# Windowed attention on one core: value products in two sets of three PSUM banks, row sums first, and an earlier second load wave

## The chip, the cores and the metric

The kernel runs on one core of a Trainium2 chip. A core has a matrix engine (TensorE, PE in the profile; its weight loads are listed as PEld), a vector engine (VectorE, DVE), a scalar engine (ScalarE, ACT), GpSimd (POOL) and SyncE (SP). They run their own instruction streams and meet at semaphores. Sixteen DMA engines carry data between the DRAM of the chip (HBM) and the on-chip memory (SBUF). Matrix results land in PSUM, which has eight banks of 128 partitions by 512 fp32 values. The metric is device time in microseconds (us) of one execution; lower is better.

## The reference

Inputs q, k and v are fp32 of shape (4, 4096, 1536). The sequence is cut into windows of 64 rows; each window attends to itself only.

```python
q_w = q.reshape(B, nw, W, D)          # B=4, nw=64, W=64, D=1536
k_w = k.reshape(B, nw, W, D)
v_w = v.reshape(B, nw, W, D)
logits = np.einsum('bnwd,bnud->bnwu', q_w, k_w) * D ** -0.5
attn = np.exp(logits - logits.max(-1, keepdims=True))
attn = attn / attn.sum(axis=-1, keepdims=True)
out = np.einsum('bnwu,bnud->bnwd', attn, v_w)
```

Each of q, k, v and out has 16384 rows of 1536 fp32 values, 100.7 MB. Reading three and writing one moves 402.7 MB.

## The kernel before

**Units.** The 16384 rows are cut into N = 32 units of 512 rows. Each partition of an SBUF tile holds SLOTS = 4 rows of the unit. Loads of q, k and v go through GpSimd's DMA queue and cast to fp16 on the way (3.146 MB read, 1.573 MB written). The result of a unit is scaled into one of three fp32 tiles `outs` and stored by one 3.146 MB DMA. So in the steady state each unit asks for four DMAs of 3.146 MB on the DRAM side: q, k, store and v, in that order on the one queue.

**One unit on the engines.** PE transposes q in six groups and k in six groups (L142), always pairs of fp16 values as one fp32, into two PSUM banks `tps` in turn; DVE copies the even groups to SBUF and ACT the odd ones (`copy_out`, L219). The score products (L160) go to two banks `lts`, one for each half h of the unit. ACT takes the exponential of the 32x32 blocks (L265) into `ets`, fp16. There is no subtraction of the maximum. Then come four value products, n = 0 to 3 (n = 2h + t): each multiplies two weight blocks of `ets` by v16, with 3 column blocks j of 512, accumulated over r = 0 and 1, into three PSUM banks `ops`. One more product per n, with a column of ones, gives the row sums (`sp`). DVE takes the reciprocal of the sums (L241); the scaled eviction of the six (n, j) with n + j even is on ACT (L276), of the other six on DVE (L250).

**Banks.** All four value products write the same three banks `ops`. The first matmul into a bank (r = 0) waits on `f_o[j][n % 2]`, which the eviction of the product before gives back (`told`). The eight banks are: two `tps`, two `lts`, three `ops`, one `sp`.

**Order of DMA work.** It is written out by hand on POOL and SP. For unit u, POOL waits for `m_q` (a small matmul after the last q transpose of the unit, L151) and issues the load of q for u+1; waits for `m_k` (a score product after the last k transpose) and issues the load of k; waits for `m_0` (value product n = 0 of the unit has begun its second half) and issues the store of unit u-1; waits for `m_v` (last value matmul) and issues the load of v. SP waits for the loads in order and hands each to PE (`g_q`, `g_k`, `g_v`).

**Start.** SP loads q of unit 0 raw (fp32) in two DMAs of two slots each into `outs[0]`; DVE and ACT cast it. When the first of the two has landed (`d_r0`), POOL issues k and v of unit 0, makes the identity matrix, and issues q, k, v of unit 1 and v of unit 2, some of them into spare halves of `outs`, from where POOL later copies them (`unstage`, L290).

**End.** v of the last unit is loaded early into `vs` and copied by DVE (L238). The store of unit 30 waits for `n_e`, a mark that DVE and ACT set after unit 30. The last unit is stored in five pieces: half h = 0 (1.573 MB) after `m_2`, slot 2 (0.786 MB) after `m_3`, both on POOL's queue, and slot 3 in three pieces of 0.262 MB from SP (L402), one after each eviction.

Of the kernel before, what the change touches and what calls it, by code (L numbers as in the profile page):

```python
# [11 lines left out]
P = 128  # L12
# [5 lines left out]
def kernel(  # L18
# [31 lines left out]
    def sem(name):  # L50
# [21 lines left out]
    d_r0, d_r1, d_q, d_k, d_v, d_vs, d_q1, d_k1, d_v1 = (  # L72
        sem(n) for n in ("d_r0", "d_r1", "d_q", "d_k", "d_v", "d_vs", "d_q1", "d_k1", "d_v1")
    )
    d_o = [sem(f"d_o{i}") for i in range(NO)]
    d_l = [sem(f"d_l{i}") for i in range(5)]
# [3 lines left out]
    f_o = [[sem(f"f_o{j}{i}") for i in range(2)] for j in range(NJ)]  # L80
# [6 lines left out]
    m_q, m_k, m_v, m_0, m_2, m_3 = (sem(n) for n in ("m_q", "m_k", "m_v", "m_0", "m_2", "m_3"))  # L87
# [44 lines left out]

    def tensor_unit():
        def transpose(g):
            src = q16 if g < DC else k16
            c = g % DC
            for i in range(SLOTS):
                r, j = i // H, i % H
                pairs = src[:, R * j + r, :].bitcast(FP32)
                if g % DC == 0 and i == 0:  # L140
                    await_(nc.tensor, g_k if g else g_q)
                ins = nc.tensor.transpose(  # L142
                    tps[g % 2][:, r, j, :], pairs[:, c * P : (c + 1) * P], ident[:, :]
                )
                if i == 0 and g >= 2:
                    ins._wait_ge(f_c[(g - 2) % 4], 1).then_inc(f_c[(g - 2) % 4], -1)
                if i == SLOTS - 1:
                    ins.then_inc(p_t[g % 2], 1)
            if g == DC - 1:

                nc.tensor.matmul(  # L151
                    lts[0][:, 0, 0, 0:1], lhsT=ets[0][:, 0, 0, :], rhs=ones[:, 0:1],
                    start=True, stop=True, skip_group_check=True,
                ).then_inc(m_q, 1)

        def product(c):
            for h in range(H):
                for w in range(2):
                    for r in range(R):
                        ins = nc.tensor.matmul(  # L160
                            lts[h][:, r, :, :],
                            lhsT=halves(xk, c)[:, r, h, :, w],
                            rhs=halves(xq, c)[:, :, h, :, w],
                            start=(c == 0 and w == 0 and r == 0),
                            stop=(c == DC - 1 and w == 1),
                            skip_group_check=True,
                        )
                        if h == w == r == 0 and c >= DC - 2:
                            s = f_c[(DC + c) % 4]
                            ins._wait_ge(s, 1).then_inc(s, -1)  # L170
                        if h == w == r == 0 and c == DC - 3:
                            ins.then_inc(m_k, 1)
                        if c == DC - 1 and w == r == 1:
                            ins.then_inc(p_l, 1)

        for g in range(2 * DC):
            transpose(g)
            if g >= DC + 2:
                product(g - DC - 2)
        product(DC - 2)  # L180
        product(DC - 1)
        for n in range(H * R):
            h, t = n // R, n % R
            if n == 0:
                await_(nc.tensor, g_v)
            for r in range(R):
                w = ets[h][:, r, t, :]
                ld = nc.tensor.ldweights(w)  # L188
                if r == 0 and t == 0:
                    ld._wait_ge(f_x[h], 1)  # L190

                at = NJ - 1 if n == H * R - 1 else 1
                for j in range(NJ):
                    ins = reuse(
                        ops[j][:, :], w, v16[:, R * h + r, 512 * j : 512 * (j + 1)], r == 0, r == R - 1
                    )
                    if r == 0:
                        ins._wait_ge(f_o[j][n % 2], 1).then_inc(f_o[j][n % 2], -1)
                    elif j > at:
                        ins.then_inc(p_o[on_act(n, j)], 1)  # L200
                    elif j == 0 and n != 1:
                        ins.then_inc({0: m_0, 2: m_2, 3: m_3}[n], 1)
                    elif j == NJ - 1:
                        ins.then_inc(m_v, 1)
                    if j == at:
                        ins = reuse(sp[:, n : n + 1], w, ones[:, 0:1], r == 0, r == R - 1)
                        if r == 0 and t == 0:
                            ins.then_inc(f_x[h], -1)
                        if r == R - 1:
                            ins.then_inc(p_s, 1)  # L210
# [4 lines left out]
    def copy_out(eng, copy, g):  # L215
        xt = xq if g < DC else xk
        await_(eng, p_t[g % 2])
        dst = xt[:, g % DC, :].rearrange("p (r e j) -> p r j e", r=R, j=H)
        copy(out=dst, in_=tps[g % 2][:, :, :, :]).then_inc(f_c[g % 4], 1)  # L219
# [5 lines left out]
    def told(ins, u, n, j, a):  # L225
        if u == N - 1 and n == H * R - 1:
            ins.then_inc(n_e[a], 1)
        else:
            ins.then_inc(f_o[j][(n + 1) % 2], 1)

    def vector_unit(u):
        ve = nc.vector
        for g in range(0, 2 * DC, 2):
            copy_out(ve, ve.tensor_copy, g)
        if u == N - 1:
            ve.wait_ge(d_vs, 32)
            ve.wait_ge(m_v, N - 1)
            ve.tensor_copy(out=v16[:, :, :], in_=vs[:, :, :]).then_inc(g_v, 1)  # L238
        for n in range(H * R):
            await_(ve, p_s)  # L240
            ve.reciprocal(out=rs[:, n : n + 1], in_=sp[:, n : n + 1]).then_inc(n_d, 1)  # L241
            await_(ve, n_d)
            ve.sem_inc(n_r, 1)  # L243
            if n == 0:
                await_(ve, fr[0])
            for j in range(NJ):
                if not on_act(n, j):
                    if j == NJ - 1 and n != H * R - 1:
                        await_(ve, p_o[0])
                    ins = ve.tensor_scalar_mul(  # L250
                        scaled(u, n, j), ops[j][:, :], scalar1=rs[:, n : n + 1]
                    )
                    told(ins, u, n, j, 0)
        if u == N - 2:
            ve.memset(zeros[:, 1:2], 0.0).then_inc(n_e[0], 1)

    def scalar_unit(u):
# [12 lines left out]
        for n in range(H * R):  # L270
            await_(sc, n_r)
            for j in range(NJ):
                if on_act(n, j):
                    if j == NJ - 1:
                        await_(sc, p_o[1])
                    ins = sc.activation(  # L276
                        scaled(u, n, j), ops[j][:, :], COPY, bias=0.0, scale=rs[:, n : n + 1]
                    )
                    told(ins, u, n, j, 1)
        if u == N - 2:  # L280
            sc.copy(out=zeros[:, 2:3], in_=zeros[:, 0:1]).then_inc(n_e[1], 1)
# [12 lines left out]
    with tc.tile_critical(no_gpsimd_drain=True):  # L294

        raw = rows(qf, 0, SLOTS, SLOTS).rearrange("p h (r d) -> p (h r) d", d=D)
        for i, s in enumerate((d_r0, d_r1)):
            sl = slice(2 * i, 2 * i + 2)
            nc.sync.dma_start(out=outs[0][:, sl, :], in_=raw[:, sl, :]).then_inc(s, 16)
        nc.gpsimd.wait_ge(d_r0, 16)  # L300
        load("k", 0, k16, d_k)
        load("v", 0, v16, d_v)
        nc.vector.memset(ident[:, :], 0.0).then_inc(i_d, 1)
        nc.gpsimd.wait_ge(i_d, 1)
        nc.gpsimd.affine_select(
            out=ident[:, :], in_=ident[:, :], compare_op=mybir.AluOpType.not_equal,
            fill=1.0, base=0, pattern=[[-1, P]], channel_multiplier=1,
        ).then_inc(i_p, 1)
        load("q", 1, staged(2, 0), d_q1)
# [12 lines left out]
        for a, eng in enumerate((nc.vector, nc.scalar)):  # L322
            copy = nc.scalar.copy if a else nc.vector.tensor_copy
            for i in range(a, SLOTS, 2):
                eng.wait_ge(d_r1 if i > 1 else d_r0, 16)
# [13 lines left out]
        for j in range(NJ):  # L339
            sy.sem_inc(f_o[j][0], 1)  # L340
# [26 lines left out]
        for u in range(1, N - 1):  # L367
            gp.wait_ge(m_q, u + 1)
            load("q", u + 1, q16, d_q)
            if u == 1:  # L370
                gp.wait_ge(d_v1, 16)
                gp.wait_ge(m_v, 1)
                unstage(staged(1, 0), v16, g_v)
            gp.wait_ge(m_k, u + 1)
# [3 lines left out]
            gp.wait_ge(m_0, u + 1)  # L378
            store(u - 1)
# [7 lines left out]
        for a in range(2):  # L387
            gp.wait_ge(n_e[a], 1)
# [3 lines left out]
        u, base, o = N - 1, (N - 1) * UR, outs[(N - 1) % NO]  # L392
        gp.wait_ge(m_2, N)
        gp.dma_start(out=rows(of, base, R, R), in_=slots(o, 0, R, R)).then_inc(d_l[0], 16)
        gp.wait_ge(m_3, N)
        half = of[base + R * P : base + UR].rearrange("(p r) d -> p r d", r=R)
        gp.dma_start(out=half[:, 0, :], in_=o[:, R, :]).then_inc(d_l[1], 16)
        gp.drain()
        for j, (a, c) in enumerate(((0, 2), (1, 2), (0, 3))):
            sl = slice(512 * j, 512 * (j + 1))  # L400
            sy.wait_ge(n_e[a], c)
            sy.dma_start(out=half[:, 1, sl], in_=o[:, R + 1, sl]).then_inc(d_l[2 + j], 16)  # L402
# [3 lines left out]
        for i in range(5):  # L406
# [36 lines left out]
```

The softmax here doesn't subtract the row's maximum and nothing guards it: scores larger than these inputs give would overflow.

## Time and profile before

| What | Value |
|---|---|
| Time, median of 6 runs | 948.4 us (947.4 to 949.37) |
| Profiled execution, its own time | 947.7 us |
| Its span, first to last instruction | 945.9 us |
| PE, ACT, DVE, POOL busy | 68%, 36%, 31%, 10% of the span |
| DMA issues, whole units | k 31, q 30, v 29 of 1536 KB (SBUF side); stores 31 of 3072 KB |
| Granted PE clock, mean | 0.903 |

The page of a profile gives the busy time of each engine, the span cut into 40 slices, the DMA queues with the time that their packets took, the chain of work that ended last, and the costliest groups of instructions. A group reads "line, engine, operation, output<-input, shape, count, busy time and mean of one, idle time before it and what ended most of it". Other views of the same trace list instructions in order of time, or the busy time of each engine in chosen stretches. In the stretches the column "DMA share" is the mean busy share of the 16 DMA engines, and GB/s counts the bytes written: a casting load writes half of what it reads, so a stretch of loads shows half the figure of a stretch of stores. Requests overlap a little on a DMA engine, so shares slightly over 1 occur. The trace also records, for each transfer, when each of its 16 parts had landed, and for each DMA packet its queue, size, start and duration.

### The profile page before, as it was taken

To read this page: it belongs to the slowest core of one execution; us is meant where nothing else is said; L and a number is where in the kernel's file an instruction comes from. 1 tells how busy PE (TensorE), PEld (TensorE's weight loads), DVE (VectorE), ACT (ScalarE), POOL (GpSimd) and SP (SyncE) were. 2 spreads that over 40 slices of the span, in tenths; PEclk is the share of its full clock that TensorE was granted. 3 is DMA by queue.
4 is the path that set the end of the run, shared out by engine and by line. 5 is a ranking of instruction groups with operands and counts; after the bars stand their busy time and mean duration, and the time that the engine had idled before them with its cause. 6 is when DMAs were issued, how large, how long until landed. Compare 5 with 4: busy or idle time off the path is not lost. (4 is left out here: it accounts for less than half of the span.)

```text
span 945.9 us, 11112 instructions
## 1 busy us (share of the span) xinstructions
PE 638.5 (68%) x4128; PEld 359.0 (38%) x3360; DVE 294.2 (31%) x521; ACT 337.1 (36%) x645; POOL 92.1 (10%) x137
## 2 busy tenths in 40 slices
PE   2677777576676577676776766677677665666863
PEld 2344444234443234424344323444234442334431
DVE  2333333323233223333233323223232333322332
ACT  2443333334324334323343334333343333333243
POOL 1221100000100001000010001001010100001100
PEclk9999999979979988969799979889697999999798
DMA  9999999999999999999999999999999999999998
GB/s 254 216 217 257 278 282 280 281 236 263 283 279 280 246 255 282 282 280 259 241 282 282 280 272 235 276 282 279 280 239 265 282 281 281 251 249 282 281 247 336
DMA packets 27225, 253.32 MB, mean 268 GB/s; under 512 B 2128, under 2 KB 2128, under 8 KB 10832
## 3 DMA queue, kind: packets, MB, share of 16 engines
q0 software_dynamic: 26496, 249.31, 100.4%
q1 hardware_dynamic: 720, 3.93, 1.1%
q14 instruction: 8, 0.07, 0.0%
q8 instruction: 1, 0.02, 0.0%
HBM read 301.99 MB, written 100.66 MB: 426 GB/s over the span
## 5 line engine op out<-in xcount | busy, mean ns | idle before, releaser
L117 PE MATMUL o<-v,et 128*128 128x512 f16 x768 | 248.4, 445 | 185.2 <-ACT out L276 68.9
L276 ACT ACTIVATE out<-o,rs 128x512 f32<-128x512 f32 x192 | 124.9, 684 | 266.0 <-ACTq L213 266.0
L160 PE MATMUL lt<-xq,xk 128*128 128x256 f16 x1536 | 195.0, 275 | 0.0
L142 PE MATMUL tp<-ident,q 128*128 128x128 f32 x768 | 116.9, 302 | 84.1 <-DVE xq L219 71.5
L188 PEld LDWEIGHTS <-et 128*128 128x128 f16 x256 | 25.4, 99 | 388.9 <-issue 360.0
L160 PEld LDWEIGHTS lt<-xq,xk 128*128 128x128 f16 x1536 | 148.4, 97 | 23.2
L250 DVE TENSOR_SCALAR out<-o,rs 128x512 f32<-128x512 f32 x192 | 138.2, 748 | 34.6 <-DVEq L213 34.6
L241 DVE RECIPROCAL rs<-sp 128x1 f32<-128x1 f32 x128 | 21.5, 168 | 404.4 <-DVEq L213 404.4
L142 PEld LDWEIGHTS tp<-ident,q 128*128 128x128 f32 x768 | 94.7, 156 | 120.9 <-issue 120.8
L142 PE MATMUL tp<-ident,k 128*128 128x128 f32 x768 | 118.6, 287 | 28.4 <-DVE xk L219 14.6
L219 ACT COPY xk<-tp 128x512 f32<-128x512 f32 x96 | 59.1, 615 | 159.4 <-ACTq L213 159.4
L265 ACT ACTIVATE et<-lt,zeros 32x128 f16<-32x128 f32 x256 | 91.8, 358 | 56.3 <-ACTq L213 53.1
L142 PEld LDWEIGHTS tp<-ident,k 128*128 128x128 f32 x768 | 91.8, 147 | 43.4 <-issue 41.4
L219 DVE COPY xk<-tp 128x512 f32<-128x512 f32 x96 | 66.5, 692 | 127.2 <-DVEq L213 127.2
L219 ACT COPY xq<-tp 128x512 f32<-128x512 f32 x96 | 59.1, 616 | 110.8 <-ACTq L213 110.7
L219 DVE COPY xq<-tp 128x512 f32<-128x512 f32 x96 | 66.1, 689 | 68.4 <-DVEq L213 68.4
L110 POOL DMA_DIRECT2D v<-in_v_dram x29 | 20.8, 716 | 259.0 <-PE o L117 259.0
L117 PE MATMUL sp<-ones,et 128*128 128x1 f16 x256 | 45.8, 179 | 0.0
L284 POOL DMA_DIRECT2D out_dram<-out x31 | 22.1, 713 | 185.8 <-PE o L117 175.6
L110 POOL DMA_DIRECT2D k<-in_k_dram x31 | 17.0, 549 | 193.7 <-PE lt L160 186.7
L110 POOL DMA_DIRECT2D q<-in_q_dram x30 | 16.3, 542 | 147.7 <-PE lt L151 141.4
L151 PE MATMUL lt<-ones,et 128*128 128x1 f16 x32 | 5.7, 179 | 0.0
(27 smaller groups left out, 29.3 us busy)
## 6 DMA issues: line engine op xcount, KB each, us to landing
out_dram<-out POOLq DMA_DIRECT2D x31, 3072.0 KB, 20.1
k<-in_k_dram POOLq DMA_DIRECT2D x31, 1536.0 KB, 18.7
q<-in_q_dram POOLq DMA_DIRECT2D x30, 1536.0 KB, 18.4
v<-in_v_dram POOLq DMA_DIRECT2D x29, 1536.0 KB, 17.6
out<-in_q_dram SPq DMA_DIRECT2D x2, 1536.0 KB, 7.8
vs<-in_v_dram POOLq DMA_DIRECT2D x2, 1536.0 KB, 35.2
out<-in_q_dram POOLq DMA_DIRECT2D x1, 1536.0 KB, 25.3
out<-in_k_dram POOLq DMA_DIRECT2D x1, 1536.0 KB, 32.0
```

Of the source, the lines that this page charges most:

```text
L110: nc.gpsimd.dma_start(out=slots(dst, 0, SLOTS, r), in_=rows(src, u * UR, SLOTS, r)).then_inc(s, 16)
L117: return nc.tensor.add_instruction(mybir.InstMatmult(name=nc.get_next_instruction_name(), engine=PE, ins=[low(rhs), low(w)], outs=[low(o)] ...
L142: ins = nc.tensor.transpose(tps[g % 2][:, r, j, :], pairs[:, c * P : (c + 1) * P], ident[:, :])
L151: nc.tensor.matmul(lts[0][:, 0, 0, 0:1], lhsT=ets[0][:, 0, 0, :], rhs=ones[:, 0:1], start=True, stop=True, skip_group_check=True,).then_in ...
L160: ins = nc.tensor.matmul(lts[h][:, r, :, :], lhsT=halves(xk, c)[:, r, h, :, w], rhs=halves(xq, c)[:, :, h, :, w], start=(c == 0 and w == 0 ...
L188: ld = nc.tensor.ldweights(w)
L219: copy(out=dst, in_=tps[g % 2][:, :, :, :]).then_inc(f_c[g % 4], 1)
L241: ve.reciprocal(out=rs[:, n : n + 1], in_=sp[:, n : n + 1]).then_inc(n_d, 1)
L250: ins = ve.tensor_scalar_mul(scaled(u, n, j), ops[j][:, :], scalar1=rs[:, n : n + 1])
L265: ins = sc.activation(ets[h][s, :, :, s], lts[h][s, :, :, s], EXP, bias=zeros[s, 0:1], scale=scale)
L276: ins = sc.activation(scaled(u, n, j), ops[j][:, :], COPY, bias=0.0, scale=rs[:, n : n + 1])
L284: nc.gpsimd.dma_start(out=rows(of, u * UR, SLOTS, R), in_=slots(outs[u % NO], 0, SLOTS, R)).then_inc(d_o[u % NO], 16)
```

## The change

The value products n = 0 and n = 2 now write to three banks that are free at that time (the two of `tps` and the first of `lts`), n = 1 and n = 3 to `ops` (`bank`). The tokens `f_o` become one for each (j, n); the next unit's first transposes and first score product wait for the evictions of n = 2. Within each half h the order on PE is: the two sums of t = 1, then the sums and products of t = 0, then the products of t = 1; six weight loads in place of four. One reciprocal serves both sums of a half.

The marks for POOL move: `m_q` and `m_k` are given by the copying engine once the last transposes of q or k are done (the small matmul at L151 is gone), `m_v` by DVE at its last eviction, and `m_0`, `m_2`, `m_3` are gone. The store of unit u-1 is issued directly after the load of q for u+1, ahead of the load of k; the order of one unit on the queue is then q, store, k, v. The store of unit 30 waits for `m_q` of the last unit.

At the start, raw q comes in three DMAs of one, one and two slots, and POOL waits for the first; it makes the identity before it issues k and v. At the end the last unit is stored in two halves of 1.573 MB, the first by POOL after the evictions of n = 0 and 1 and one of n = 2 on each engine, the second by SP after all.

```diff
+    def bank(n, j):
+        if n % 2:
+            return ops[j][:, :]
+        t = (*tps, lts[0])[j]
+        return t[:, :, :, :].rearrange("p a b c -> p (a b c)")
...
-        for n in range(H * R):
-            h, t = n // R, n % R
-            if n == 0:
-                await_(nc.tensor, g_v)
-            for r in range(R):
+        await_(nc.tensor, g_v)
+        for h in range(H):
+            for t, r, what in (
+                (1, 0, "s"), (1, 1, "s"), (0, 0, "sv"), (0, 1, "sv"), (1, 0, "v"), (1, 1, "v")
+            ):
+                n = R * h + t
...
     def copy_out(eng, copy, g):
         xt = xq if g < DC else xk
         await_(eng, p_t[g % 2])
+        if g % DC == DC - 1:
+            eng.sem_inc(m_q if g < DC else m_k, 1)
...
-            await_(ve, p_s)
-            ve.reciprocal(out=rs[:, n : n + 1], in_=sp[:, n : n + 1]).then_inc(n_d, 1)
-            await_(ve, n_d)
-            ve.sem_inc(n_r, 1)
+            if n % R == 0:
+                await_(ve, p_s)
+                ve.reciprocal(out=rs[:, n : n + R], in_=sp[:, n : n + R]).then_inc(n_d, 1)
+                await_(ve, n_d)
+                ve.sem_inc(n_r, 1)
...
-        for i, s in enumerate((d_r0, d_r1)):
-            sl = slice(2 * i, 2 * i + 2)
+        for sl, s in ((slice(0, 1), d_r0), (slice(1, 2), d_r1), (slice(2, SLOTS), d_r2)):
             nc.sync.dma_start(out=outs[0][:, sl, :], in_=raw[:, sl, :]).then_inc(s, 16)
-        nc.gpsimd.wait_ge(d_r0, 16)
-        load("k", 0, k16, d_k)
-        load("v", 0, v16, d_v)
         nc.vector.memset(ident[:, :], 0.0).then_inc(i_d, 1)
         nc.gpsimd.wait_ge(i_d, 1)
+        nc.gpsimd.wait_ge(d_r0, 16)
         nc.gpsimd.affine_select(
...
         ).then_inc(i_p, 1)
+        load("k", 0, k16, d_k)
+        load("v", 0, v16, d_v)
...
+            if u + 1 < N - 1:
+                store(u - 1)
             gp.wait_ge(m_k, u + 1)
             load("k", u + 1, k16, d_k)
             if u + 1 == N - 1:
                 load("v", u + 1, vs, d_vs)
-            gp.wait_ge(m_0, u + 1)
-            store(u - 1)
+                store(u - 1)
...
-        for a in range(2):
-            gp.wait_ge(n_e[a], 1)
+        gp.wait_ge(m_q, N)
         store(N - 2)
-        gp.wait_ge(m_2, N)
-        gp.dma_start(out=rows(of, base, R, R), in_=slots(o, 0, R, R)).then_inc(d_l[0], 16)
-        gp.wait_ge(m_3, N)
-        gp.dma_start(out=half[:, 0, :], in_=o[:, R, :]).then_inc(d_l[1], 16)
+        for h, (eng, c) in enumerate(((gp, 1), (sy, 3))):
+            for a in range(2):
+                eng.wait_ge(n_e[a], c)
+            eng.dma_start(
+                out=rows(of, base + R * P * h, R, R), in_=slots(o, R * h, R * h + R, R)
+            ).then_inc(d_l[h], 16)
         gp.drain()
-        for j, (a, c) in enumerate(((0, 2), (1, 2), (0, 3))):
-            sl = slice(512 * j, 512 * (j + 1))
-            sy.wait_ge(n_e[a], c)
-            sy.dma_start(out=half[:, 1, sl], in_=o[:, R + 1, sl]).then_inc(d_l[2 + j], 16)
```

## Prediction

> **What bounds the kernel now.** I read the page's DMA lines first, then the stretches, then who waited for whom, and last the order of time on POOL and SP at the start and the end.
>
> ```profile
> DMA  9999999999999999999999999999999999999998
> ...
> q0 software_dynamic: 26496, 249.31, 100.4%
> ...
> HBM read 301.99 MB, written 100.66 MB: 426 GB/s over the span
> ```
>
> All 40 slices are at 90% or more, and the packets of one queue fill 16 engines for 100.4% of the span (a little over, since requests overlap). PE is busy for 68%. The stretches sharpen it (columns: length, busy time of PE, PEld, DVE, ACT, POOL, PE clock, DMA share, GB/s written):
>
> ```profile
> 2.00:10.00 8.00, 0.00 (x0) 0.00 (x0) 0.96 (x1) 1.96 (x3) 2.48 (x5) 1.00 0.99 386
> ...
> 300.00:600.00 300.00, 209.29 (x1346) 117.74 (x1105) 93.36 (x165) 106.40 (x204) 25.65 (x41) 0.89 1.02 272
> ...
> 932.00:934.00 2.00, 1.34 (x8) 0.19 (x2) 0.68 (x3) 0.24 (x1) 0.57 (x1) 1.00 0.52 221
> 934.00:942.00 8.00, 1.63 (x8) 0.10 (x1) 2.06 (x4) 1.71 (x3) 0.55 (x1) 0.88 0.96 389
> ```
>
> The DMA engines are full from 2 us on; the one hole worth the name is at 932 to 934, 0.48 x 2 = 1.0 us. The landings say the same: in the middle, transfers of 3.146 MB land 7.26 to 7.36 us apart, 29.17 us a unit, whatever the engines do. 128 such transfers take 933 us; packets run from 1.97 to 943.6 us, so some 8.6 us are lost inside, in 2.4 us around the first k load, in three slow spots (landings late by 1.7, 1.0 and 0.8 us at 73, 96 and 272 us), and in small change.
>
> Compute waits for data, as SP's queue shows (total, times, longest):
>
> ```profile
> SPq L358 <- DMA v<-in_v_dram: 415.6, 29, 14.7
> ```
>
> That is 14.3 us in each of 29 units. Next, how early POOL issues (start, length):
>
> ```profile
> 872.08 0.71 POOL L284 DMA_DIRECT2D out_dram<-out  x1 [6.46 <-PE o L117]
> 883.92 0.71 POOL L110 DMA_DIRECT2D v<-in_v_dram  x1 [11.13 <-PE o L117]
> 889.38 0.54 POOL L110 DMA_DIRECT2D q<-in_q_dram  x1 [4.75 <-PE lt L151]
> 896.28 0.54 POOL L110 DMA_DIRECT2D k<-in_k_dram  x1 [6.35 <-PE lt L160]
> ```
>
> The tightest is v: issued at 883.92, when the store ahead of it lands its first part at 888.96 and its last at 892.58. So there is always about a transfer in hand. The start and the end are the only places where the change can touch the time directly:
>
> ```profile
> 0.96 0.86 SPq L299 DMA_DIRECT2D out<-in_q_dram  x2
> ...
> 7.46 0.81 POOL L110 DMA_DIRECT2D k<-in_k_dram  x1 [7.02 <-DMA out<-in_q_dram]
> ...
> 75.60 0.56 POOL L110 DMA_DIRECT2D q<-in_q_dram  x1 [3.75 <-PE lt L151]
> ...
> 933.25 0.57 POOL L394 DMA_DIRECT2D out_dram<-out  x1 [20.25 <-PE o L117]
> 936.06 0.55 POOL L397 DMA_DIRECT2D out_dram<-out  x1 [2.24 <-PE o L117]
> ...
> 937.55 2.42 SPq L402 DMA_DIRECT2D out_dram<-out  x3
> ```
>
> **1. Value products.** In the last unit the first value matmul starts at 926.21 and the last eviction ends at 938.18, 12.0 us: four rounds in which PE waits for an eviction. A block of three matmuls and a sum takes 0.68 us there (926.21, next block 926.67 and 927.34 for the halves of it), so eight blocks and the leading sums need 5.7 us with no bank to wait for. DVE evicts six at 0.75, 4.5 us, and behind the last matmul come an eviction's latency and two evictions (in the trace 936.37 to 938.18). That gives 7.2 us, 4.8 us less per unit. The two added weight loads (0.10 us) lie beside matmuls; the 32 small matmuls of L151 (0.18 us) go. On the path that sets the end all this counts 0: it lies under the DMA queue. Where that cover is gone, a unit is worth at most the 4.8 us.
>
> **2. Waits added on PE.** The next unit's first transposes wait for the evictions of n = 2, which end while n = 3 runs (2.0 us of matmuls); behind that wait stand transposes, then `m_q`, then a load with over 5 us in hand. The sum at h = 1 waits for the eviction of (0, 0), done 2.3 us after the first value matmul, PE being busy to 2.8. Both 0. ACT's loop grows by three semaphore steps a unit, DVE's and PE's hardly change. The first copies in the loops began 4.2 us (ACT) and 5.6 us (DVE) after the last cast; should a loop's jump cost ACT 4.2 us once in three units, the 9 us of item 3 cover it.
>
> **3. New order q, store, k, v.** Count from the landing of v of unit u as 0. k landed at -7.3 now (the store moved ahead of it); 9.0 us of k transposes and score products (915.95 to 924.94), 1.6 us to the exponential's first half, 5.7 us of value products and an eviction for `m_v`: v of the next unit is issued at about 10. Ahead in the queue are q, store and k, 21.9 us of transfers, so the engines want it by about 19.9: 9 us in hand, where before the value phase of 13.3 us (870.58 to 883.92) left 6.6. q is issued at 15, wanted at 27; store directly behind it; k at 27, wanted at 42. Cost 0, gain 0, since a full queue can't be fuller. If a margin went negative, each microsecond would come back in up to 31 units.
>
> **4. Start.** The first of two raw q transfers landed at 7.17, the second 3.67 later, so a quarter lands near 7.17 - 1.83 = 5.3. Then POOL's identity (0.32) comes first and k is issued at about 5.9 in place of 7.46; 1.5 us earlier, v and the four others with it. Before, k's first packet ran at 10.10, just as q's ran out (last end 10.48); between 10.25 and 11.0 the engines were short by 0.1 us in the mean, 0.5 on the worst. That hole closes. Against it stand 8 packets of 6144 B in two transfers (236 ns, so 3.78 us an engine) in place of 12288 B (460 ns, 3.68): +0.1. I take -0.25 + 0.1 = -0.15, ends -0.6 and +0.3.
>
> The price is hidden at first: k shares the engines with the second half of q. k can't start before 7.0 (the 1.1 us from issue to first packets at 933.25) or after 8.5 (the 2.6 us of 7.46 to 10.10). If packets alternate, 460 ns of q to 926 ns of k, q gets a third: the 3.4 or 1.9 us still to run become 10.3 or 5.8, and q lands 3.9 to 6.9 us later than 10.84. That packets of both queues move together is seen at the end, where SP's three small stores landed within 5.3 to 5.6 us while POOL's were still running. Unit 0 slips by X = 4 to 7. What is late next: PE runs units 0 and 1 back to back, so q of unit 3 is issued at 75.6 + X, less 4.2 us (in PE's time; 10.0 down to 5.8) for each of two value phases: 71 to 74. The same three transfers stand ahead of it; the last of them landed its first part at 76.8, some 0.5 us after its packets, and 1.1 go from issue to packet, so it is wanted by 75.2 (before, it was 0.4 late for the first engines). From X = 8.0 on it costs. q of unit 2, 48.51 + X - 4.2 = 48.2 to 51.2, is wanted by 52.7. So X costs 0 here; if the software queue had all six loads served first, q would land with the last of them at 56.5 and cost some 38 us, which the row at the end speaks against.
>
> The Trainium skill ("DMA: Bandwidth & Descriptors", Queues, rings and completion order) says that a DMA engine goes round its queue rows packet by packet; the row of the end agrees, and the estimate by it is the same X.
>
> **5. End.** Order and positions of the last six transfers stay (k, v, store 29, store 30, two halves). Value products of the last unit start at 926.2 as before, since k lands at 914.5 either way. The first half is released at about 931.5 (before 933.25), the second at 933.4 by SP, as all evictions end 7.2 us after the start. Some DMA engines lag and run store 30 until about 934.8 without a break, so the hole at 932 to 934 closes only for those ahead: the two last engines ended at 943.6, most others by 942.3, and these had the hole. For the two last only packets change: 24 of 2048 B (85 ns) and 8 of 6144 B (240 ns) make 3.96 us; 8 of 12288 B make 3.68. Term -0.28, ends -1.3 (all as early as the others) and +0.5.
>
> A rule speaks against the coarse end. The Trainium skill ("DMA: Bandwidth & Descriptors", Anatomy of one DMA) puts a transfer at 2.0 us + bytes / 436 GB/s: an exposed last piece of 1.573 MB instead of 0.262 would cost 3.0 us more. Here the last piece of 0.262 MB took 5.4 us to land, being queued behind others, and the new last piece is queued too.
>
> **Sum.** -0.15 - 0.28 = -0.4 us on the profiled 947.7: 947.3. This execution lies 0.7 under the median of 948.4, so the median becomes 948.0.
>
> **Rivals.** (a) *No change to speak of* is my forecast. For it: DMA share 1.02 over 300 us. (b) *Faster*: the three slow spots came in the units where q of unit 3 was late, or while stores and loads of the old order met; if the new order spares them, 3.5 us go with the 0.4, to 944.5. If only the end balances, 947.0. Against it: packets there were long (1.4 to 2.4 us for 0.93) on engines that had work. (c) *Slower, by a starved raw q*: if q gets a quarter or less of the engines, X is 10.2 and more (3.4 us drawn out to 13.6); from 8.0 on each us costs one: +2.2, 950.2; a fifth gives X = 13.6 and +5.6, 953.6. For it: unit 0 is what everything hangs on, and no row shows both queues with long loads. (d) *Slower, by the end*: if the second half is released after 938, the engines run dry and the 1.573 MB stand alone, +3.0 by 3.7 us of packets less 0.7 for the old last piece: 951.0. It takes 4.6 us of lateness.
>
> **How the numbers follow.** About 0.2% (1.9 us) is what a measurement of this kernel can tell from no change. Chances: forecast 0.56; faster 0.22; (c) 0.14; (d) or an unseen stall in the loop 0.08. Range: from (b) at 944.5 to 951.5, past (d) and a quarter's share in (c); what it leaves out is the far part of (c) and a stall. The forecast's own range, from the ends of items 4 and 5, is 946.5 to 949.2.
>
> **What would show it.** After: DMA share 1.0 in 300 to 600 us, landings 29.17 us a unit; value phase near 7 us; k issued near 5.9 and raw q landed at 14 to 18; q of unit 3 issued by 74; no hole at 932; the last SP store issued near 933.4. I am wrong if shares under 0.98 appear in 10 to 100 us, or if landings in the middle spread.

## The result and the profile after

The changed kernel takes 951.0 us (median of 17 runs, 949.88 to 952.7). The kernel before, run beside it, takes 948.48 us (median of 38 runs, 946.54 to 953.13). The ratio is 1.0022, 95% interval 1.0012 to 1.0032: slower by 0.22%. The profiled execution took 950.87 us with a span of 949.1, against 947.7 and 945.9: 3.2 us more in the span.

The page after, its DMA lines:

```profile
DMA  9999999999999999999999999999999999999996
...
q0 software_dynamic: 26352, 248.52, 99.9%
...
HBM read 301.99 MB, written 100.66 MB: 424 GB/s over the span
```

They say the same as before, with a weaker last slice. The stretches after (columns as before: length, busy time of PE, PEld, DVE, ACT, POOL, PE clock, DMA share, GB/s written):

```profile
2.00:10.00 8.00, 0.00 (x0) 0.00 (x0) 0.96 (x1) 1.97 (x3) 4.06 (x7) 1.00 1.00 387
...
300.00:600.00 300.00, 191.95 (x1281) 124.26 (x1082) 86.24 (x140) 102.90 (x200) 25.27 (x40) 0.84 1.02 268
600.00:900.00 300.00, 197.67 (x1318) 129.08 (x1118) 87.65 (x142) 104.13 (x202) 24.54 (x39) 0.84 1.02 268
900.00:932.00 32.00, 26.72 (x196) 14.89 (x153) 15.64 (x24) 17.49 (x35) 3.22 (x5) 1.00 0.97 277
932.00:934.00 2.00, 0.00 (x0) 0.00 (x0) 0.00 (x0) 0.00 (x0) 0.00 (x0) 1.00 0.99 424
934.00:942.00 8.00, 0.00 (x0) 0.00 (x0) 0.00 (x0) 0.00 (x0) 0.00 (x0) 0.60 0.93 396
942.00:949.10 7.10, 0.00 (x0) 0.00 (x0) 0.00 (x0) 0.00 (x0) 0.00 (x0) 0.50 0.03 14
```

In the middle the DMA share is 1.02, as before, yet GB/s written over 300 to 900 us fell from 270 to 268. First the kernel before, then the changed one:

```profile
300.00:900.00 600.00, 414.72 (x2668) 232.00 (x2187) 184.46 (x325) 212.56 (x410) 51.99 (x83) 0.89 1.02 270
```

```profile
300.00:900.00 600.00, 389.62 (x2598) 253.34 (x2199) 173.88 (x282) 207.03 (x402) 49.81 (x79) 0.84 1.02 268
```

The hole at 932 to 934 is closed (0.52 before, 0.99 now). A new one lies in 900 to 932; at a mean of 0.97 it is worth about 1 us, as much as the closed one. The last stretch is new in kind: 7 us in which nearly nothing moves. Its share of 0.03 is that of one engine out of 16 busy for 3.4 us.

POOL in the last units and SP's longest wait (start, length; total, times, longest):

```profile
871.72 0.56 POOL L110 DMA_DIRECT2D k<-in_k_dram  x1 [13.52 <-ACTq L222]
880.77 0.70 POOL L110 DMA_DIRECT2D v<-in_v_dram  x1 [8.50 <-DVEq L256]
885.29 0.56 POOL L110 DMA_DIRECT2D q<-in_q_dram  x1 [3.82 <-ACTq L222]
901.71 0.53 POOL L110 DMA_DIRECT2D k<-in_k_dram  x1 [15.86 <-ACTq L222]
```

```profile
SPq L361 <- DMA k<-in_k_dram: 437.2, 31, 14.7
```

Compute still waits for data, 14.1 us a unit; it now waits for k, which comes behind the store, and no longer for v.

The end, on POOL and SP, and what SP waited for there:

```profile
930.98 0.57 POOL L399 DMA_DIRECT2D out_dram<-out  x1 [14.91 <-ACT out L281]
```

```profile
932.00 0.35 SPq L399 DMA_DIRECT2D out_dram<-out  x1
```

```profile
SPq L407 <- DMA out_dram<-out: 13.3, 1, 13.3
SPq L297 <- POOLq L297: 2.2, 1, 2.2
```

Both halves are issued early. SP then waits 13.3 us for the last of them, to 945.65. That is not the end of its wait: another 2.2 us go in waiting for POOL, whose queue is closed by a drain. Before, the same wait was 0.6 us (the line is L294 there).

**Where the 3.2 us are.** The trace records when each of a transfer's 16 parts landed. How far the last part comes behind the median part is called the lag below. I count the large transfers behind raw q and give, for some of them, when the last part landed and (in brackets) the median part, in us:

| | transfer 40 | transfer 120 | last landing | end of span |
|---|---|---|---|---|
| before | 308.6 (306.3) | 892.6 (889.6) | 944.1 | 945.9 |
| after | 305.9 (304.5) | 893.0 (887.8) | 945.7 | 949.1 |
| difference | -2.7 | +0.4 | +1.6 | +3.2 |

So the changed kernel is 2.7 us ahead after ten units. Over the next 80 transfers it loses 3.1 (587.1 against 584.0). To the last landing it loses 1.2 more (52.7 against 51.5 us), and from there to the end of the span 1.6 (3.4 against 1.8). The 1.2 us stand in one transfer, the load of v for the last unit: its last part lands 8.5 us after that of the transfer ahead, and so does the median part, where before both took 7.3. Between 916.4 and 919.3 us, 41 of its packets of 6144 B took more than 560 and up to 1474 ns, where 474 is usual. This is not the drift described next, since all engines lose it.

The 3.1 us are not in the bulk: the median part needs 583.3 us (583.2 before) for those 80 transfers in both kernels. In the changed kernel one DMA engine alone falls behind the others:

| last part behind the median part, near | 350 us | 526 us | 702 us | 878 us |
|---|---|---|---|---|
| before | 2.3 | 2.3 | 2.6 | 2.8 |
| after | 1.4 | 2.75 | 3.9 | 5.0 |

The second-latest part stays 1.5 behind the median after. The drift is about 0.2 us a unit (3.6 us in 18 units), and it is made in the stores: between 300 and 880 us 97 of about 5,100 store packets of 12288 B took over 476 ns ("long" below; their median is 484) where 460 is usual. Together they ran 2.8 us longer than 460 ns each would make, most of the 3.6 us by which the lag grew. Before, 64 such packets ran 1.8 us longer, in engines that were not yet the last. The packets of loads did not change (926 and 474 ns). A transfer is done when its last part is, so the one engine sets the pace of the chain.

### The profile page after: what moved, and what is told of

It reads as the page before. It is cut to its first block, busy times and chain, and to the rows that moved or that the text cites. A ratio compares the mean times of both kernels' runs of the same rounds, so it can differ in the third digit from the quotient of the medians.

```text
span 949.1 us, 11240 instructions
## 1 busy us (share of the span) xinstructions
PE 608.6 (64%) x4096; PEld 392.7 (41%) x3456; DVE 280.7 (30%) x456; ACT 333.8 (35%) x644; POOL 92.1 (10%) x136
## 5 line engine op out<-in xcount | busy, mean ns | idle before, releaser
L149 PE MATMUL tp<-ident,k 128*128 128x128 f32 x768 | 153.8, 347 | 229.1 <-PEq L215 222.0
L149 PEld LDWEIGHTS tp<-ident,k 128*128 128x128 f32 x768 | 119.4, 181 | 249.8 <-issue 247.2
L161 PE MATMUL lt<-xq,xk 128*128 128x256 f16 x1536 | 214.1, 291 | 0.0
L117 PE MATMUL o<-v,et 128*128 128x512 f16 x384 | 93.3, 379 | 0.0
L257 DVE TENSOR_SCALAR out<-o,rs 128x512 f32<-128x512 f32 x128 | 90.2, 746 | 7.7
L117 PE MATMUL tp<-v,et 128*128 128x512 f16 x256 | 75.8, 377 | 0.0
L281 ACT ACTIVATE out<-tp,rs 128x512 f32<-128x512 f32 x64 | 44.0, 687 | 35.9 <-ACTq L215 31.3
L257 DVE TENSOR_SCALAR out<-tp,rs 128x512 f32<-128x512 f32 x64 | 48.0, 751 | 26.2 <-DVEq L215 26.2
L117 PE MATMUL lt<-v,et 128*128 128x512 f16 x128 | 48.3, 378 | 0.0
L281 ACT ACTIVATE out<-o,rs 128x512 f32<-128x512 f32 x64 | 44.0, 688 | 0.0
```

The costliest lines, as they stand in the source:

```text
L117: return nc.tensor.add_instruction(mybir.InstMatmult(name=nc.get_next_instruction_name(), engine=PE, ins=[low(rhs), low(w)], outs=[low(o)] ...
L149: ins = nc.tensor.transpose(tps[g % 2][:, r, j, :], pairs[:, c * P : (c + 1) * P], ident[:, :])
L161: ins = nc.tensor.matmul(lts[h][:, r, :, :], lhsT=halves(xk, c)[:, r, h, :, w], rhs=halves(xq, c)[:, :, h, :, w], start=(c == 0 and w == 0 ...
L257: ins = ve.tensor_scalar_mul(scaled(u, n, j), bank(n, j), scalar1=rs[:, n : n + 1])
L281: ins = sc.activation(scaled(u, n, j), bank(n, j), COPY, bias=0.0, scale=rs[:, n : n + 1])
```

## The experiments

Five explanations were put up: the place of the store on the queue by itself (number 1 where an expectation gives numbers), POOL's issuing of the store right behind a load (2), its issuing of the v load while the store runs (3), what PE and the copying engines do beside the store, the q transposes above all (5), and, as the rival that would make the question idle, that the loss is all at the end of the program, by the last half on POOL's queue and its drain. Ratios are to the kernel before, run on the same chip in turn with the experiment. The sets ran on three chips, and its median differed between them, 947.84, 949.29 and 950.21 us; a difference in us across sets can be off by that much, the ratios are safer. Where an expectation reckons with a drift of 0.17 us a unit, the trace gives about 0.2 (29.36 us a unit for the last parts, 29.16 for the median part).

### The store behind k again

```diff
-            if u + 1 < N - 1:
-                store(u - 1)
             gp.wait_ge(m_k, u + 1)
             load("k", u + 1, k16, d_k)
+            if u + 1 < N - 1:
+                store(u - 1)
```

> The changed kernel, but POOL issues the store of unit u-1 directly after the load of k instead of after the load of q; the queue order is q, k, store, v again, everything else as changed. Theory 1 (order on the queue): a DMA engine that lags does its store while the others run the next transfer; beside loads of q or k (24 KB packets) a store packet takes 476 ns, beside loads of v 460. With v next, the lag should stay under 3 us, units take 29.17 us from 350 to 850 us, and the median falls from 951.0 by about 3 to 948. Theory 2 (issue): the lag grows because POOL now writes the descriptors of a store right behind those of a load; that stays, so units stay at 29.34 us, the lag passes 4 us and the median stays at 951.

Measured: 945.2 us (944.31 to 945.96), ratio 0.9965 (0.995 to 0.998). Eight store packets over 476 ns instead of 97, the lag constant at 2.9 us, 80 transfers in 583.3 us, the last landing at 940.8. So all of the rest of the change, with the old order of the queue, is a gain of 0.35%, and the new place of the store costs 5 to 6 us. In the profiled executions it is 5.1: 3.8 in the 80 transfers, 0.9 from there to the last landing (v of the last unit takes 7.3 us again), the rest in small change. In this run, too, the store is issued right behind a load, and there is no drift, so explanation 2 is out. Span minus last landing stays long, 3.2 us.

### The old kernel with the store ahead of k

```diff
+            if u + 1 < N - 1:
+                store(u - 1)
             gp.wait_ge(m_k, u + 1)
             load("k", u + 1, k16, d_k)
             if u + 1 == N - 1:
                 load("v", u + 1, vs, d_vs)
-            gp.wait_ge(m_0, u + 1)
-            store(u - 1)
+                gp.wait_ge(m_0, u + 1)
+                store(u - 1)
```

> The kernel before, with one move: the store of unit u-1 is issued directly after the load of q, ahead of the load of k (its wait for m_0 goes; the store of unit 29 stays where it was). Theory 1 (order on the queue): one DMA engine starts to drift by 0.17 us a unit once it is about 1.5 us late, units become 29.34 us, the last part of a load lands 4 us or more behind the median part by 850 us, and the median rises from 948.5 to 950.5 to 952. If the drift is due to the shorter value products or the start instead, the median stays at 948.5 and units at 29.17 us.

Measured: 955.6 us (954.61 to 958.26), ratio 1.0078 (1.006 to 1.0095). It is slower, but not by the drift: six long store packets, the lag constant at 2.1 us, 80 transfers in 583.4 us. It loses in the first units (transfer 40 lands at 312.5 against 308.6) and at the end, where the last evictions come late. POOL and the stretches of this kernel:

```profile
941.18 0.57 POOL L396 DMA_DIRECT2D out_dram<-out  x1 [20.25 <-PE o L117]
```

```profile
932.00:940.00 8.00, 4.38 (x26) 0.99 (x11) 2.32 (x5) 4.82 (x11) 0.00 (x0) 1.00 0.69 295
```

Store 30 has landed by 939.8, before the first half of the last unit is issued: the engines are dry (0.69), which is what rival (d) of the prediction described. So the order alone does not make an engine drift. That it is the short value phase which spares the changed kernel these losses is likely, but no run tests it by itself.

### The last half by SP

SP issues both halves of the last unit here.

```diff
-        for h, (eng, c) in enumerate(((gp, 1), (sy, 3))):
+        for h, (eng, c) in enumerate(((sy, 1), (sy, 3))):
```

> The changed kernel, with both halves of the last unit issued by SP, so that POOL's queue ends with the store of unit 30. Theory: POOL's drain ends 2.2 us after the last transfer of its own queue has landed (947.86 after 945.67 in the changed kernel, 944.63 after 942.46 before), and only then come the closing steps. With store 30 landing near 941, the drain is over before the last landing near 945.5, and the span ends 1.8 us after it in place of 3.4: median 949.4. Rival: the drain hides nothing, the time stays at 951.0 within 0.4.

Measured: 948.86 us (947.66 to 950.87), ratio 1.0002 (0.9991 to 1.0014), 2.1 us under the changed kernel (1.9 by the ratios). The drift is there (lag 0.55 to 4.0 us, 93 long packets), and the last landing is no earlier, 946.1; but the span ends 1.3 us after it instead of 3.4. Its waits of SP at the end, all of them:

```profile
SPq L398 <- ACT out L281: 16.6, 2, 15.9
SPq L407 <- DMA out_dram<-out: 13.1, 2, 9.5
SPq L438 <- PEq L438: 0.5, 2, 0.4
SPq L399 <- DVE out L257: 0.4, 1, 0.4
```

The wait for POOL of 2.2 us is gone. Who issues the last transfer costs 2 us here, though the same bytes land no earlier.

### Both

The two edits together.

> Both edits: store behind the load of k, and both last halves from SP. If the two causes are separate and are all of it, the effects add: 951.0 - 3 - 1.6 = 946.4, below the kernel before. If the lag is the only cause, as in the run with the store behind k alone.

Measured: 943.71 us (943.07 to 944.07), ratio 0.9947 (0.9931 to 0.9962). The last landing is at 940.9, the end of the span at 942.2, six long packets. This version beats both kernels; its page:

```profile
q0 software_dynamic: 26208, 246.95, 100.0%
...
HBM read 301.99 MB, written 100.66 MB: 427 GB/s over the span
```

The two edits nearly add up: 5.8 us for the order, 2.1 for the end, 7.3 together (951.0 to 943.71); on top of the old order the end brings 1.5 (945.2 to 943.71). The share of the queue is what it was before (100.0% against 100.4), while GB/s went from 424 to 427.

### v issued behind the store

The changed kernel, with POOL held until the store has landed, so that it issues nothing while it runs:

```diff
             elif u + 1 < N - 1:
                 gp.wait_ge(m_v, u + 1)
+                gp.wait_ge(d_o[(u - 1) % NO], 16 * ((u - 1) // NO + 1))
                 load("v", u + 1, v16, d_v)
```

> The changed kernel with its queue order q, store, k, v, but POOL waits until the store of unit u-1 has landed before it issues the load of v; no DMA is issued while that store runs, and v still has most of k's 7.3 us in hand. Theory 1 (order): the lagging DMA engine's store packets are slowed because k runs beside them; unchanged here, so the lag still grows by 0.17 us a unit and the median stays near 951. Theory 3 (issue during the store): the slow store packets (476 to 502 ns for 460) appear in the traces only where POOL issues a DMA while the store runs (v in the changed kernel at 528.8 in a store of 522 to 534; q at 537.1 in a store of 532 to 541 in the kernel before; none in the two kernels with the store behind k, nor in the old kernel with the store ahead). Then the lag stays under 2 us, units take 29.17 us and the median falls by 2.5 to 4, to 947 to 948.5.

Measured: 951.32 us (950.25 to 952.72), ratio 1.002 (1.0006 to 1.0034). POOL did wait:

```profile
886.57 0.71 POOL L110 DMA_DIRECT2D v<-in_v_dram  x1 [13.54 <-DMA out_dram<-out]
```

and the long packets stayed, 94 of them; no DMA was issued in any of the 20 stores from 300 to 880 us. The 80 transfers took 586.0 us. Here the median part needed 584.9, 1.6 more than in the changed kernel, and the lag grew only from 2.0 to 3.0, because the other engines lost time as well: 55 packets of loads took over 1000 ns there, 2 in the changed kernel. The stores were slowed all the same. POOL's issuing beside the store is not the cause.

### v issued into the store

The reverse, on the version with the store behind k: the load of v waits until k has landed, and so falls into the store.

```diff
                 gp.wait_ge(m_v, u + 1)
+                gp.wait_ge(d_k, 16 * (u + 1))
                 load("v", u + 1, v16, d_v)
```

> The changed kernel with the store behind k (945.2 us), but POOL waits until k of the next unit has landed before it issues v; the issue then falls into the run of the store (about 1 us after its start, for one of 7.3 us). Theory 1 (order: store followed by v doesn't drift): 945.2 within 0.6 and a steady lag. Theory 3 (issue during the store): one engine's store packets go to 476 to 502 ns, its lag grows by 0.1 to 0.3 us a unit, and the median rises to 948 to 952.

Measured: median 945.83 us, but 12 runs from 944.17 to 960.05: eight at 944 to 946, four at 955 to 960. Ratio 0.9985 (0.9951 to 1.0018), without the run at 960.05. The profiled execution, one of the lower group, shows 39 long packets and one engine's lag going from 0.6 to 2.4 us; 80 transfers took 584.0 us. Issuing into the store makes at most a weak drift. What happened in the other four was not traced.

### Both, with the old start

The version of "Both" with raw q in two transfers and k issued ahead of the identity matrix, as before.

```diff
-        for sl, s in ((slice(0, 1), d_r0), (slice(1, 2), d_r1), (slice(2, SLOTS), d_r2)):
+        for sl, s in ((slice(0, 2), d_r0), (slice(2, SLOTS), d_r2)):
             nc.sync.dma_start(out=outs[0][:, sl, :], in_=raw[:, sl, :]).then_inc(s, 16)
+        nc.gpsimd.wait_ge(d_r0, 16)
+        load("k", 0, k16, d_k)
+        load("v", 0, v16, d_v)
...
-        nc.gpsimd.wait_ge(d_r0, 16)
...
-        load("k", 0, k16, d_k)
-        load("v", 0, v16, d_v)
         load("q", 1, staged(2, 0), d_q1)
```

> The kernel with both edits (store behind k, last halves from SP; 943.7 us), but with the start of the kernel before: raw q in two transfers, k and v of unit 0 issued when half of q has landed, the identity behind them. If the earlier second wave is worth the 0.7 us by which v of unit 2 lands earlier in the changed kernel's profile (55.8 for 56.5), the median is 944.4. If the start is worth nothing, 943.7; if a later raw q cost more than the earlier wave gained, less than 943.7.

Measured: 944.24 us (943.9 to 944.43), ratio 0.9943 (0.9921 to 0.9964), against 0.9947 for "Both". The medians, from different sets, differ by 0.5 us the other way, so a worth of 0.7 us can't be told from nothing: the new start brings nothing that can be measured. Transfer 40 lands at 306.2, 2.4 us ahead of before, with the old start and the old order of the queue. So that early gain comes from the rest of the change: the second set of banks and the earlier marks, with which POOL issues q of unit 3 at 69.52 instead of 75.60.

### q handed over behind the store

The changed kernel, with the same order of the queue. SP hands q of a unit to PE only when the store beside which its transposes would run has landed.

```diff
+            if NO <= u < N - 1:
+                sy.wait_ge(d_o[(u - 2) % NO], 16 * ((u - 2) // NO + 1))
```

> The changed kernel with its order q, store, k, v, but SP hands q of a unit to PE only after the store that runs behind that load has landed (units 3 to 30); k lands 7.3 us later still, so the wait should hide. In the changed kernel and the two variants with its order, 89 to 96% of the store packets over 476 ns start while PE transposes q. Theory 5 (the q transposes and their copies beside the store slow one DMA engine): the lag stays under 2 us, 80 transfers from 306 to 893 us take 583 to 584 us in place of 587, the median falls from 951.0 to about 948. If the coincidence means nothing, 587 and 951.

Measured: 945.97 us (945.13 to 948.86), ratio 0.9956 (0.9935 to 0.9977). SP's waits of this kernel show the added wait as the long one:

```profile
SPq L363 <- DMA out_dram<-out: 405.7, 28, 15.1
SPq L363 <- DMA k<-in_k_dram: 229.5, 31, 14.6
```

An added wait ahead of q, in units 3 to 30, made the kernel 5 us faster (6 by the ratios). PE stands still for 5.5 us between the value products and the next q transposes (876.4 to 881.9 in one of the last units), while the rest of the store runs, and compute had that time to spare. There are 16 long packets, the lag stays near 2.0 us up to 880 us, 80 transfers take 583.5. The order is that of the changed kernel, and POOL issued v inside each of the 20 stores from 300 to 880 us, so in this order the drift needs what runs on the compute engines beside the store. The load of v for the last unit takes 7.3 us again. The last landing is at 940.5, and the drain is still paid: the span ends 3.4 us later.

### The store behind v

The version of "Both" with the store as the last of the four.

```diff
-            if u + 1 < N - 1:
-                store(u - 1)
             if u + 1 == N - 1:
                 load("v", u + 1, vs, d_vs)
...
                 load("v", u + 1, v16, d_v)
+            if u + 1 < N - 1:
+                store(u - 1)
```

> The kernel with the store behind k and both last halves from SP (943.7 us), with the store moved once more, behind the load of v: the order is q, k, v, store. Theory 1 (a store followed by a load of q or k drifts, one followed by v doesn't): the store now has q behind it, so 80 transfers take about 587 us in place of 583.3 and the median is near 947. If only the place between q and k is bad, 583.3 and 943.7.

Measured: 948.14 us (946.86 to 949.06), ratio 0.998 (0.9963 to 0.9998). The drift is back (107 long packets, lag 2.6 to 5.0 us, 80 transfers in 585.7), although no q transpose runs beside the store.

### What the runs settle, and what stays open

Worked out from the trace's packet records between 300 and 880 us: the share of store packets that had such PE work within 0.3 us of them.

| kernel | long packets | beside all store packets | beside the long ones |
|---|---|---|---|
| before | 64 | q transposes 65%, k transposes 33% | k transposes 94% |
| after | 97 | value products 77%, q transposes 26% | q transposes 100% |
| v behind the store | 94 | value products 77%, q transposes 38% | q transposes 97% |
| store behind v | 107 | score products 89%, k transposes 57% | value products 64%, score products 36% |
| store behind k | 8 | k transposes 64%, score products 30% | |
| old kernel, store ahead | 6 | value products 96%, q transposes 1% | |
| q behind the store | 16 | value products 58%, then nothing | value products 100% |

Settled: most of the 5 to 6 us (3.8 of 5.1 in the profiled executions) is one DMA engine's, whose long store packets take some 25 ns more than usual; the place of the store in the new kernel brings them, and keeping the q transposes out of it takes them away. The granted PE clock is not behind it: it fell from 0.903 to 0.856 with the change, and is 0.857 with the store behind k, where nothing drifts. Not settled is what makes those packets longer. In each kernel the long packets lie beside one or two kinds of work, but not the same kind: the long ones lie beside q transposes in the changed kernel and not in the old one, where most store packets run beside them. In the kernels with over 60 long packets at least 94% of them came in the second half of a store, when other engines may already be at the next transfer, which may be what counts; no run tests that. Nor is it known why v of the last unit is slow: its long packets stand in the changed kernel, with the last half by SP and with v behind the store (8.5, 8.7 and 8.5 us), and not in the other runs (7.3).

The Trainium skill ("DMA: Bandwidth & Descriptors", Latency and other measured facts) notes that two of the 16 DMA engines are usually slower than the rest, and guesses at the memory port on which GpSimd's descriptors lie. That one engine is slower is seen here; which one, the trace doesn't name, and a port can't be shown by these runs.

## Why the prediction was wrong

The prediction said no change to speak of, 948.0 us, with 0.56. The kernel became slower by 0.22%, beyond its interval. The time of 951.0 lies inside the range of 944.5 to 951.5, but by none of the rivals. Rival (d) had that very number, which is luck: its condition, a second half released after 938, was not met (932.0). Nearest is the "unseen stall in the loop", which shared 0.08 with (d) and had no mechanism. One of the two signs of being wrong did appear: landings in the middle spread.

**1, value products: right.** In the last unit, first and last lines of the phase:

```profile
925.30 0.21 PE L117 MATMUL sp<-ones,et 128*128 128x1 f16 x3 [0.81 <-PEq L215]
...
930.56 1.41 DVE L257 TENSOR_SCALAR out<-o,rs 128x512 f32<-128x512 f32 x2
930.87 0.69 ACT L281 ACTIVATE out<-o,rs 128x512 f32<-128x512 f32 x1
```

From 925.30 to 931.97 it is 6.7 us, for 7.2 predicted and 12.0 before. (The two terms named there, 5.7 and the 1.8 from 936.37 to 938.18, would make 7.5.)

**2, waits on PE: right.** PE did not become the bound; it is busy for 64% of the span instead of 68%.

**3, the order q, store, k, v: the step that failed.** "Cost 0, gain 0, since a full queue can't be fuller" took the mean over 16 engines for the bound. The queue stayed as full. But what ends a transfer is its last part, and one engine needed about 0.2 us a unit more than the others: 3.1 us in 80 transfers, against before. With the store put back behind k the kernel takes 945.2 us, so the cost put at 0 was 5 to 6. The trace of before held the sign: the last part landed 2.3 to 2.8 us behind the median part there, three steps between landings in the middle were 7.5 to 7.6 us, outside the 7.26 to 7.36 that the prediction read, and it spoke of engines that "lag" at the end itself. It did not ask what sets that lag.

The 9 us of margin were sound for v. For k, "at 27, wanted at 42" counts a store ahead of it; in the last turn the kernel issues that store behind k, so that only q stands ahead, and the issue of k also hangs on the last part of the k before it. It came at 901.71 (896.28 before), and for the engines that were ahead the queue ran dry for a moment (first before, then after):

```profile
900.00:910.00 10.00, 6.43 (x34) 0.86 (x10) 3.42 (x7) 4.41 (x9) 0.72 (x1) 1.00 1.02 217
```

```profile
900.00:910.00 10.00, 9.25 (x68) 4.18 (x45) 3.74 (x7) 5.90 (x13) 1.94 (x3) 1.00 0.88 173
```

Median parts of k of the last unit landed 9.0 us after those of the transfer ahead, instead of 7.3. The lagging engine had no pause there (7.3 us), so at this place the hole cost nothing by itself. The transfer behind it, v of the last unit, cost all engines 1.2 us, as said above; whether the hole has to do with that is open.

**4, the start: the mechanism right, sizes off, no gain that could be measured.**

```profile
5.94 0.83 POOL L305 TENSOR_SCALAR_AFFINE_SELECT ident<-ident 128x128 f32<-128x128 f32 x1 [5.50 <-DMA out<-in_q_dram]
6.73 0.68 POOL L110 DMA_DIRECT2D k<-in_k_dram  x1
...
70.25 0.54 POOL L110 DMA_DIRECT2D q<-in_q_dram  x1 [7.67 <-ACTq L222]
```

The identity took 0.8 us instead of 0.3, so k was issued at 6.73, not 5.9. Raw q had landed by 13.0, which makes X about 2 us, not 4 to 7: by the prediction's own sum it kept more than a third of the engines. q of unit 3 was issued at 70.25, before the 74 that was asked for. Rival (c) is out. The sign given for (c), shares under 0.98 from 10 to 100 us, is absent (1.00 to 1.04). The experiment with the old start shows no gain.

What rival (b) hoped for did come about: the first ten units gained 2.7 us, of which 0.7 by transfer 6 (55.8 against 56.5), the rest between there and 306 us, where the slow spots were smaller (0.9, 0.35 and 0.85 us late, for 1.7, 1.0 and 0.8). Item 3 ate it up.

**5, the end: half right.** Releases (930.98 and 932.00, for 931.5 and 933.4) and the closed hole were as predicted. From the landing of store 29 to the last landing it took 14.6 us, for 14.9 before, close to the -0.28. But the working stopped at the landing. The last landing moved from SP's pieces to POOL's half, which stood behind store 30 on the lagging engine; POOL's drain ends 2.2 us after the landing of its own last transfer in both kernels, and that was hidden before, where POOL's last landing came at 942.46 and SP's at 944.1. From the last landing to the end that is +1.6, which the prediction has no term for, and about 2 by the run with both halves on SP.

The rule that the prediction weighed there, the Trainium skill's 2.0 us + bytes / 436 GB/s ("DMA: Bandwidth & Descriptors", Anatomy of one DMA), would by an estimate have made the coarse last piece cost 3.0 us; the page gives it for transfers issued by GpSimd, and the old and the new last piece are SP's. In the version with both edits, transfer 120 to the last landing takes 51.6 us (889.3 to 940.9), and 51.5 before: the coarse pieces, queued behind others, cost nothing that shows.

**Sum.** Predicted -0.15 and -0.28. Measured in the profile: -2.7 (early units), +3.1 (drift in 80 transfers), +1.2 (v of the last unit; a little more drift and the -0.28 cancel), +1.6 (drain), together +3.2.

## What to carry to other kernels

When a DMA queue is full, look at the latest of the engines and not at the mean share: compare the last part's landing with the median part's over the whole span, and a lag that grows is time lost, though every share reads 1.0. Try the places of a long store among the loads on the chip, since what runs beside it changes the packets of one engine and neither the order nor the work alone foretells it. At the end of a program count on to the last instruction: the same transfer cost 1.5 to 2 us less issued by SP than by GpSimd, whose drain comes after the landing.

## What was not expected of the hardware

- One DMA engine's store packets of 12288 B take up to 507 ns instead of 460 in the changed kernel, beside certain compute, while the median load packets keep 926 and 474 ns. Some five long packets a store made most of a drift of about 0.2 us a unit.
- GpSimd's drain ends 2.2 us after the landing of the last transfer of its own queue (944.63 for 942.46 before, 947.86 for 945.67 after).
- Holding compute back made the kernel faster: an added wait on SP, before q, took 951.0 to 945.97 us.
- The kernel before scatters over 946.2 to 955.4 us in these sets, while the versions with both edits keep within 1 us. Its profiled execution has a second engine whose lag grows from 0.3 to 3.1 us and stays just hidden behind the latest. Whether its longer runs are those in which it shows was not traced.
